# Moving the split of w_o from the scan's chunks to the w_in products, with more buffers for the chunks

## The chip, the cores and the metric

The kernel runs on one core of a Trainium2 chip. The metric is device time in microseconds (us), from the first to the last instruction of the core and what lies around it; the time before is the median of three runs.

## The reference

One decoder layer is computed for a prompt of 1024 rows and for 64 sample rows (8 sequences of 8), together T = 1088 columns. All is fp32.

```
h = rmsnorm(x) * (1 + scale) + shift                       # scale, shift, gate from silu(c) @ w_ada
[u_pool | z_pool | z_ssm | xBC | dt | g] = h @ w_in
P = (pool_mix(u_pool) * silu(z_pool)) @ w_pool_out
S = gated_rmsnorm(SSD(conv(xBC)) + D*x, z_ssm) @ w_ssm_out
x = x + gate * ((sigmoid(g_pool) * P + sigmoid(g_ssm) * S) @ w_o)
y = rmsnorm(x)
```

SSD is the scan of Mamba-2: 32 heads in 4 groups, in chunks of 128 rows, with a state that is handed from chunk to chunk. Beside y, the new pooling, convolution and scan states are written.

## The kernel before, in words

TensorE multiplies in fp32r. To keep the precision, each factor is split into a high part (a copy to fp32r by ScalarE, `act(hi, raw, AF.Copy)`) and a low part (the difference raw - hi), and each product is made of three matmuls: high by high, high by low, low by high. So each weight is split before it is used.

The stages follow each other:

- Up to about 100 us: x is normed and transposed, and the modulation is made.
- The w_in products, about 100 to 820 us. A pair of column blocks of w_in is multiplied by Strassen's scheme in seven products (`strassen`, L603 to L605). The weight blocks are split in `split`: the high part whi on ScalarE (L160), the low part wlo on GpSimd (L163), with four buffers each. Sums and differences of weights run on VectorE and GpSimd (L549), the convolution on VectorE (L1051). In the first part, the generator `splits` runs beside the products: it is stepped once a product and splits w_pool_out (8 jobs) and w_ssm_out (32 jobs, with a gain of each row put on by four ScalarE operations, L429). A job loads a 128x512 block into the tile pw (L421), makes the high half in the tile ph and stores it (L430, L431), makes the low half on GpSimd in place (L432), and stores it (L436), into tensors wp and ws in device memory. In the last part of the stage the samples' scan runs beside the products.
- The chunks, about 830 to 1110 us: 32 chunks (4 groups of 8) of the scan, between which the products with w_pool_out (`P_unit`, L1618) and w_ssm_out (`S_unit`, L1636, L1639) are woven in. The order of TensorE is written out by `in_line`; a planner orders the other engines and SyncE's queue by its own simulated times.
- The tail, from about 1110 us: the last group's products, the merge by the gates, the product with w_o (L1892 to L1894), and the last norm.

`chunk` is a generator with these steps: it loads xb (the convolved rows) and dec (the decays, L1182); makes cE and the exponentials (L1392, L1187, L1196); loads sz, transposes x and B, and makes xd (x times dt, L1412), xw and its low part xwl (the weighted x, L1415, L1419), bt and btl (B, L1406, L1420), and weighs dec and cE (L1416, L1418); then TensorE applies them (L1208, L1211) and updates the state (L1429 to L1431), and `finish` gates the result. The loop over i calls the first step three chunks ahead, the second two, the third one.

In this loop the generator `wo_splits` is stepped twice per chunk from the fourteenth chunk of the loop on, and what is left of it runs after the loop (the planner puts its instructions earlier: the first load starts at 839.9 us): 16 halves of w_o are loaded (L1668) and split (L1674, L1676), and stored to the tensors wo (L1675, L1670), from which the tail loads them. Its tile pw has two buffers, its ph one; both lie in the chunks' pools.

Tiles are named by tag, and the number of buffers of a tag is given where it is allocated. Loads are issued by SyncE (`load`), most stores by ScalarE (`store_`), each engine's queue in order: an instruction that waits holds what stands behind it. `behind` and `tc.issue_after` hold an instruction back in the planner's order until another was issued.

Of the kernel before, what the change touches and what calls it, by code (L numbers as in the profile page):

```python
# [8 lines left out]
F32 = mybir.dt.float32  # L9
F32R = mybir.dt.float32r  # L10
AF = mybir.ActivationFunctionType
ALU = mybir.AluOpType
# [8 lines left out]
P = 128  # L21
D = 1024
# [3 lines left out]
NS = 64  # L26
# [3 lines left out]
NG = 4  # L30
# [16 lines left out]
def tile_pool_ssd_step(  # L47
# [6 lines left out]
    nc = tc.nc  # L54
    uid = [0]

    def nm(s):
        uid[0] += 1
        return f"{s}_{uid[0]}"
# [325 lines left out]
    def dram(name, shape, dt=F32):  # L385
        return dr.tile(list(shape), dt, tag=name, name=name)
# [10 lines left out]
    wp_d = [dram(f"wp{m}", [P, 2, 4, P]) for m in range(8)]  # L397
    ws_d = [[dram(f"ws{g}{m}", [P, 2, 4, P]) for m in range(8)] for g in range(NG)]

    def behind(engine, n=0):  # L400

        of = (i for i in reversed(nc.cur_bb.bb.instructions) if i.engine == engine)
        for _ in range(n):
            next(of)
        return tc.issue_after(next(of))


    def splits():
        jobs = [(w_pool_out[0, :, m * P:(m + 1) * P], None, wp_d[m]) for m in range(8)]
        jobs += [(w_ssm_out[0, g * 512:(g + 1) * 512, m * P:(m + 1) * P], 24 + 4 * g, ws_d[g][m])  # L410
                 for g in range(NG) for m in range(8)]
        raws, made = {}, [0]

        def paced():

            return highs[min(made[0] + 3, len(highs) - 1)]

        def begin(n):
            raws[n] = gas[0].tile([P, 4, P], F32, tag="pw", name=nm("pw"), bufs=2)
            with tc.issue_after(paced()):  # L420
                store_(raws[n], jobs[n][0].rearrange("(k p) c -> p k c", p=P))  # L421

        def halve(n):
            raw, gain = raws[n], jobs[n][1]
            hi = gas[0].tile([P, 4, P], F32R, tag="ph", name=nm("ph"), bufs=1)
            with tc.issue_after(paced()):
                if gain is not None:
                    for k in range(4):
                        act(raw[:, k], raw[:, k], AF.Copy, scale=vT[:, gain + k:gain + k + 1])  # L429
                act(hi, raw, AF.Copy)  # L430
                store_(jobs[n][2][:, 0], hi.bitcast(F32))  # L431
            nc.gpsimd.tensor_tensor(raw.bitcast(F32R), raw, hi.bitcast(F32), ALU.subtract)  # L432

        def end(n):
            with behind(mybir.EngineType.SP):
                load(jobs[n][2][:, 1], raws.pop(n))  # L436
# [303 lines left out]
    gas = []  # L740
# [616 lines left out]
    def ckt(shape, tag, bufs=2):  # L1357
        return (cl if tag in CKL else ca if tag in ("dec", "xb", "cE") else ck).tile(list(shape), F32, tag=tag, name=nm(tag), bufs=bufs)
# [14 lines left out]
        nc.gpsimd.tensor_tensor(yl[g][:, :, o:o + S], v, yhc.bitcast(F32), ALU.subtract)  # L1373

    def sample_end(g):
        sz = ckt([P, 4, P], "sz", 3)[:, :, :NS]
        load(sz, z_d[g][:, :, SEQ:])
        v = ckt([P, 4, P], "v")[:, :, :NS]
        load(v, ys_d[g])
        finish(g, SEQ, NS, v, sz)  # L1380

    def chunk(g, c):
        o = c * P
        xb = ckt([P, 6, P], "xb", 3)
        load(xb, xbc_d[g][:, :, o:o + P])
        Bf, Cf = xb[:, 4], xb[:, 5]
        dec = ckt([P, 8, P], "dec", 3)
        decays(dec, g, c)
        yield
        if c > 0:  # L1390
# [21 lines left out]
        V.tensor_tensor(xd, pxv, dtT[:, c, heads].unsqueeze(2).to_broadcast([P, 8, 64]), ALU.mult)  # L1412
        V.tensor_tensor(pxv, pxv, wdT[:, c, heads].unsqueeze(2).to_broadcast([P, 8, 64]), ALU.mult)
        xwh, xwl = (ck.tile([P, 512], F32R, tag=t, name=nm(t), bufs=1) for t in ("xw", "xwl"))
        act(xwh, px, AF.Copy)  # L1415
        V.tensor_tensor(dec, dec, pbc[:, P:2 * P].unsqueeze(1).to_broadcast([P, 8, P]), ALU.mult)  # L1416
        if c > 0:
# [185 lines left out]
    ck = right.__enter__()  # L1603
# [54 lines left out]
                nxt += 1  # L1658
            yield from run(ws.pop(i))
    pc_ = pieces()  # L1660
    wo_d = [dram(f"wo{k}", [P, 2, D]) for k in range(8)]

    def wo_splits():
        raws = {}
        for n in range(18):
            if n < 16:
                raws[n] = ck.tile([P, 512], F32, tag="pw", name=nm("pw"), bufs=2)
                load(raws[n], w_o[0, n // 2 * P:n // 2 * P + P, n % 2 * 512:n % 2 * 512 + 512])  # L1668
            if n > 1:
                load(wo_d[(n - 2) // 2][:, 1, n % 2 * 512:n % 2 * 512 + 512], raws.pop(n - 2))  # L1670
            yield
            if n < 16:
                hi = ck.tile([P, 512], F32R, tag="ph", name=nm("ph"), bufs=1)
                act(hi, raws[n], AF.Copy)  # L1674
                store_(wo_d[n // 2][:, 0, n % 2 * 512:n % 2 * 512 + 512], hi.bitcast(F32))  # L1675
                nc.gpsimd.tensor_tensor(raws[n].bitcast(F32R), raws[n], hi.bitcast(F32), ALU.subtract)  # L1676
            yield
    wos = wo_splits()
    RATE = 2.56
    FRONT = 4  # L1680

# [11 lines left out]
        next(pc_)  # L1693
    next(seq[0])
    for i in range(len(seq)):
        if i > 12:
            next(wos, None)
        if i + 1 < len(seq):
            with behind(mybir.EngineType.DVE, 1 - i) if i < 2 else ExitStack():
                next(seq[i + 1])  # L1700
        products(i + 0.4)
        if i > 0:
            next(seq[i - 1], None)
        if i > 12:
            next(wos, None)
# [10 lines left out]
    for it in (pc_, wos):  # L1716
        for _ in it:
            pass
    in_line((mybir.EngineType.PE,))
    right.__exit__(None, None, None)  # L1720
    while right_all:
# [16 lines left out]
    for c in range(9):  # L1738
        n = min(P, T - c * P)
# [5 lines left out]
    for c in range(9):  # L1745
        n = min(P, T - c * P)
# [4 lines left out]
    wo, mh, ml = [None] * 8, [None] * 8, [None] * 8  # L1751
# [90 lines left out]
    for half in range(2):  # L1842
        c = slice(half * 512, half * 512 + 512)
# [102 lines left out]
```

## Time and profile before

| what | before |
|---|---|
| median of 3 runs | 1297.37 us (1296.57 to 1301.63) |
| span of the profiled execution | 1297.1 us |
| the profiled execution's own time around it | not given beside its span |
| TensorE busy | 1255.9 us (97%) |
| VectorE, ScalarE, GpSimd busy | 910.5, 708.8, 677.4 us |
| moved by DMA | 251.70 MB, mean 194 GB/s |

In the profile PE is TensorE, PEld its weight loads, DVE VectorE, ACT ScalarE, POOL GpSimd and SP SyncE; L12 is line 12 of the kernel, always of the kernel before in this part. A row of windows gives, for a stretch in us, its length, then the busy time of each engine with its count of instructions, the granted clock of TensorE, the share of the DMA engines and the rate in GB/s. A row of waits names who waited for whom, then the total in us, how often, and the longest. A row of a tile gives the least, the median and the greatest duration in ns, and the first and last start in us. A q behind an engine's name is its sequencer, which issues DMAs. The chain of waits lists start and duration in us.

### The profile page before, as it was taken

Reading aid. Unit: us, or ns where it says so; the run is one execution under the profiler, and the core shown is the slowest. Engines: PE = TensorE matmul, PEld = TensorE weight load, DVE = VectorE, ACT = ScalarE, POOL = GpSimd, SP = SyncE. Lnnn points to the kernel's source line nnn. Section 1 sums busy time; section 2 is a strip of 40 time slices with the busy share of each in tenths; the row PEclk is TensorE's granted clock in tenths of the full one; section 3 lists DMA queues with packets and bytes.
Section 4 is the critical chain, followed back from the end, with each engine's and each line's share of the span. In section 5 each row is a group of like instructions: output and inputs, shape, how many; then the busy total and the mean of one; then the engine's idle time right before and its main releaser. Section 6 shows DMA issues by size and latency. Waiting matters only on the chain.

```text
span 1297.1 us, 26554 instructions
## 1 busy us (share of the span) xinstructions
PE 1255.9 (97%) x9771; PEld 1173.9 (90%) x9771; DVE 910.5 (70%) x1580; ACT 708.8 (55%) x1684; POOL 677.4 (52%) x563
## 2 busy tenths in 40 slices
PE   7999999999999999999999999999998999999998
PEld 6779999989999999999889999889998999999786
DVE  4685778866979578775777665488676888576433
ACT  4665356375656564545455453687987868201111
POOL 1007668677869776664344444276776747314000
PEclk9999999999999999999999999999999999999999
DMA  9837345465455544444656555999988656575631
GB/s 326 259 107 224 119 150 173 142 202 170 146 180 197 165 155 133 161 135 129 181 158 173 152 178 164 356 355 354 338 270 262 202 168 199 172 266 159 226 106 52
DMA packets 233795, 251.70 MB, mean 194 GB/s; under 512 B 31265, under 2 KB 177905, under 8 KB 233658
## 3 DMA queue, kind: packets, MB, share of 16 engines
q1 hardware_dynamic: 161568, 171.60, 42.1%
q10 hardware_dynamic: 72098, 78.41, 17.5%
q8 instruction: 77, 1.26, 0.4%
q14 instruction: 52, 0.43, 0.1%
HBM read 167.06 MB, written 83.01 MB: 193 GB/s over the span
## 4 chain that ended last, share of the span: by engine, by line
PE 67%; issue 8%; DMA 8%; DVE 6%; POOL 5%; ACT 4%; SPq 0%; ACTq 0%; POOLq 0%; DVEq 0%
PE ps L603 6%; PE ps L604 6%; PE ps L605 6%; PE mm L603 6%; PE mm L605 6%; PE mm L604 6%; PE mm L355 3%; PE mm L356 3%; PE mm L354 3%; PE ps L1208 2%; PE ps L1892 2%; PE ps L1894 2%; PE ps L1893 2%; POOL wlo L163 2%; PE ps L1211 2%
## 5 line engine op out<-in xcount | busy, mean ns | idle before, releaser
L163 POOL TENSOR_TENSOR wlo<-rawA,whi 128x512 fp32r<-128x512 f32 x120 | 184.0, 1538 | 185.6 <-ACT whi L160 101.6
L163 POOL TENSOR_TENSOR wlo<-raw,whi 128x512 fp32r<-128x512 f32 x92 | 150.7, 1646 | 125.3 <-ACT whi L160 91.1
L354 PE MATMUL mm<-Y,whi 128*128 128x352 f32 (+1 forms) x480 | 160.1, 334 | 0.7 <-DVE G L1795 0.5
L355 PE MATMUL mm<-Y,whi 128*128 128x352 f32 (+1 forms) x480 | 157.3, 328 | 1.0 <-DVE Y L1466 1.0
L356 PE MATMUL mm<-Y,wlo 128*128 128x352 f32 (+1 forms) x480 | 156.9, 327 | 0.0
L605 PE MATMUL mm<-Y,wlo 128*128 128x272 f32 x496 | 143.6, 290 | 3.9 <-POOL wlo L163 3.1
L603 PE MATMUL ps<-Y,whi 128*128 128x272 f32 x496 | 144.5, 291 | 2.3 <-ACT o L803 1.7
L603 PE MATMUL mm<-Y,whi 128*128 128x272 f32 x496 | 146.5, 295 | 0.2
L604 PE MATMUL ps<-Y,whi 128*128 128x272 f32 x496 | 143.1, 289 | 0.0
L604 PE MATMUL mm<-Y,whi 128*128 128x272 f32 x496 | 142.9, 288 | 0.0
L605 PE MATMUL ps<-Y,wlo 128*128 128x272 f32 x496 | 142.6, 288 | 0.0
L160 ACT ACTIVATE whi<-rawA 128x512 fp32r<-128x512 f32 x125 | 78.2, 626 | 95.6 <-PE ps L604 44.9
L1051 DVE SCALAR_TENSOR_TENSOR GA<-GA,cvT,GA 128x1112 f32<-128x1112 f32 x72 | 127.1, 1769 | 0.6 <-ACT GA L1048 0.5
L160 ACT ACTIVATE whi<-raw 128x512 fp32r<-128x512 f32 x96 | 58.7, 626 | 91.4 <-DVE raw L549 41.7
L605 PEld LDWEIGHTS mm<-Y,wlo 128*128 128x128 f32 x496 | 93.4, 188 | 5.8 <-POOL wlo L163 4.2
L603 PEld LDWEIGHTS ps<-Y,whi 128*128 128x128 f32 x496 | 93.3, 188 | 4.0 <-ACT o L803 1.9
L603 PEld LDWEIGHTS mm<-Y,whi 128*128 128x128 f32 x496 | 93.3, 188 | 2.5 <-issue 0.8
L604 PEld LDWEIGHTS mm<-Y,whi 128*128 128x128 f32 x496 | 93.4, 188 | 0.7 <-issue 0.6
L604 PEld LDWEIGHTS ps<-Y,whi 128*128 128x128 f32 x496 | 93.3, 188 | 0.3 <-issue 0.2
L605 PEld LDWEIGHTS ps<-Y,wlo 128*128 128x128 f32 x496 | 93.4, 188 | 0.2 <-issue 0.2
L354 PEld LDWEIGHTS mm<-Y,whi 128*128 128x128 f32 x480 | 90.3, 188 | 3.2 <-DVE G L1795 1.4
L355 PEld LDWEIGHTS mm<-Y,whi 128*128 128x128 f32 x480 | 90.3, 188 | 3.2 <-DVE Y L1466 1.6
(452 smaller groups left out, 3851.6 us busy)
## 6 DMA issues: line engine op xcount, KB each, us to landing
rawA<-in_w_in SPq DMA_DIRECT2D x46, 512.0 KB
dec<-acs_d SPq DMA_DIRECT2D x32, 512.0 KB
xbc<-GA ACTq DMA_DIRECT2D x24, 512.0 KB
xb<-xbc SPq DMA_DIRECT2D x32, 384.0 KB
rawA<-in_w_in SPq DMA_DIRECT2D x32, 256.0 KB
pw<-in_w_ssm_out ACTq DMA_DIRECT2D x32, 256.0 KB
ws<-ph ACTq DMA_DIRECT2D x32, 256.0 KB
ws<-pw SPq DMA_DIRECT2D x32, 256.0 KB
```

Source lines behind the costliest of these rows:

```text
L160: ins = act(hi[:, :, :ncols], raw[:, :, :ncols], AF.Copy)
L163: (eng or nc.gpsimd).tensor_tensor(lo[:, :, :ncols], raw[:, :, :ncols], hi[:, :, :ncols].bitcast(F32), ALU.subtract)
L354: mm(ps[:, :n], a, rh[k][:, o:o + n], start=(k == 0), stop=False)
L355: mm(ps[:, :n], a, rl[k][:, o:o + n], start=False, stop=False)
L356: mm(ps[:, :n], b, rh[k][:, o:o + n], start=False, stop=(k == nk - 1))
L603: mm(p, hi, ah, start=(k == 0), stop=False)
L604: mm(p, hi, al, start=False, stop=False)
L605: mm(p, lo, ah, start=False, stop=(k == 3))
L1051: V.scalar_tensor_tensor(d[:, :n], rp[:, k:k + n], cvT[:, 24 * k + mc:24 * k + mc + 1], d[:, :n], ALU.mult, ALU.add)
L1208: mm(o[hh], xd[:S, 2 * q + hh, :], dec[:S, 2 * q + hh], start=True, stop=state is None)
L1211: mm(o[hh], state[:, h * 64:h * 64 + 64], cE[:, h], start=False, stop=True)
L1892: mm(ps[:, :cw], mhk, wo[k][0][:, s], start=(k == 0), stop=False)
```

## The change

The 16 halves of w_o are split by `splits`, as jobs 40 to 55 behind those of w_pool_out and w_ssm_out, beside the w_in products; `wo_splits` and its steps in the loop over chunks are taken out. The jobs are spaced 12/5 steps apart in place of 17/5, so that 56 of them end where 40 did, and the tile pw there has three buffers in place of two. In the chunks, xb, dec and sz get a fourth buffer, and xd, xw, xwl, bt and btl a second. The scratch memory that is reserved for dynamic DMAs is set to 1024 (`dynamic_dma_scratch_size`); before, it was left at its larger default.

```
     def splits():
-        jobs = [(w_pool_out[0, :, m * P:(m + 1) * P], None, wp_d[m]) for m in range(8)]
-        jobs += [(w_ssm_out[0, g * 512:(g + 1) * 512, m * P:(m + 1) * P], 24 + 4 * g, ws_d[g][m])
-                 for g in range(NG) for m in range(8)]
+        jobs = [(tiles(w_pool_out[0, :, m * P:(m + 1) * P]), None, [wp_d[m][:, j] for j in range(2)]) for m in range(8)]
+        jobs += [(tiles(w_ssm_out[0, g * 512:(g + 1) * 512, m * P:(m + 1) * P]), 24 + 4 * g,
+                  [ws_d[g][m][:, j] for j in range(2)]) for g in range(NG) for m in range(8)]
+        jobs += [(half(w_o[0, k * P:(k + 1) * P], n), None, [half(wo_d[k][:, j], n) for j in range(2)])
+                 for k in range(8) for n in range(2)]
...
-            raws[n] = gas[0].tile([P, 4, P], F32, tag="pw", name=nm("pw"), bufs=2)
+            raws[n] = gas[0].tile([P, 4, P], F32, tag="pw", name=nm("pw"), bufs=3)
...
-                at.setdefault(n * 17 // 5 + step, []).append((f, n))
+                at.setdefault(n * 12 // 5 + step, []).append((f, n))
...
     def chunk(g, c):
-        xb = ckt([P, 6, P], "xb", 3)
+        xb = ckt([P, 6, P], "xb", 4)
-        dec = ckt([P, 8, P], "dec", 3)
+        dec = ckt([P, 8, P], "dec", 4)
-        sz = ckt([P, 4, P], "sz", 3)
+        sz = ckt([P, 4, P], "sz", 4)
-        bth, btl = (ck.tile([P, P], F32R, tag=t, name=nm(t), bufs=1) for t in ("bt", "btl"))
+        bth, btl = (ck.tile([P, P], F32R, tag=t, name=nm(t), bufs=2) for t in ("bt", "btl"))
-        xd = ckt([P, 8, 64], "xd", 1)
+        xd = ckt([P, 8, 64], "xd", 2)
-        xwh, xwl = (ck.tile([P, 512], F32R, tag=t, name=nm(t), bufs=1) for t in ("xw", "xwl"))
+        xwh, xwl = (ck.tile([P, 512], F32R, tag=t, name=nm(t), bufs=2) for t in ("xw", "xwl"))
...
-    def wo_splits():
-        raws = {}
-        for n in range(18):
-            if n < 16:
-                raws[n] = ck.tile([P, 512], F32, tag="pw", name=nm("pw"), bufs=2)
-                load(raws[n], w_o[0, n // 2 * P:n // 2 * P + P, n % 2 * 512:n % 2 * 512 + 512])
-            if n > 1:
-                load(wo_d[(n - 2) // 2][:, 1, n % 2 * 512:n % 2 * 512 + 512], raws.pop(n - 2))
-            yield
-            if n < 16:
-                hi = ck.tile([P, 512], F32R, tag="ph", name=nm("ph"), bufs=1)
-                act(hi, raws[n], AF.Copy)
-                store_(wo_d[n // 2][:, 0, n % 2 * 512:n % 2 * 512 + 512], hi.bitcast(F32))
-                nc.gpsimd.tensor_tensor(raws[n].bitcast(F32R), raws[n], hi.bitcast(F32), ALU.subtract)
-            yield
...
-        if i > 12:
-            next(wos, None)
...
-    nc = _bacc.Bacc("TRN2", target_bir_lowering=False, num_devices=1)
+    nc = _bacc.Bacc("TRN2", target_bir_lowering=False, num_devices=1, dynamic_dma_scratch_size=1024)
```

`sample_end` gets the fourth sz as well. The destination of a half of w_o is the same as before, its high part by ScalarE's queue and its low part by SyncE's; its load is now issued by ScalarE.

More of the change, by code (lines that the diff above doesn't have):

```diff
@@ L398, in tile_pool_ssd_step @@
     ws_d = [[dram(f"ws{g}{m}", [P, 2, 4, P]) for m in range(8)] for g in range(NG)]
+    wo_d = [dram(f"wo{k}", [P, 2, D]) for k in range(8)]
     def behind(engine, n=0):
@@ L418, in begin @@
         def begin(n):
[L419 removed]
+            raws[n] = gas[0].tile([P, 4, P], F32, tag="pw", name=nm("pw"), bufs=3)
             with tc.issue_after(paced()):
[L421 removed]
+                store_(raws[n], jobs[n][0])
         def halve(n):
@@ L430, in halve @@
                 act(hi, raw, AF.Copy)
-                store_(jobs[n][2][:, 0], hi.bitcast(F32))
+                store_(jobs[n][2][0], hi.bitcast(F32))
             nc.gpsimd.tensor_tensor(raw.bitcast(F32R), raw, hi.bitcast(F32), ALU.subtract)
@@ L435, in end @@
             with behind(mybir.EngineType.SP):
-                load(jobs[n][2][:, 1], raws.pop(n))
+                load(jobs[n][2][1], raws.pop(n))
         at = {}
@@ L1715, in tile_pool_ssd_step @@
     next(seq[-1], None)
-    for it in (pc_, wos):
-        for _ in it:
-            pass
+    for _ in pc_:
+        pass
     in_line((mybir.EngineType.PE,))
```

10 lines of the change are left out of this document (5 added, 5 removed).

## The prediction
> **What bounds the kernel now.** I read the page first, for which engine fills the span.
>
> ```profile
> span 1297.1 us, 26554 instructions
> PE 1255.9 (97%) x9771; PEld 1173.9 (90%) x9771; DVE 910.5 (70%) x1580; ACT 708.8 (55%) x1684; POOL 677.4 (52%) x563
> ```
>
> TensorE is busy in 97% of the span. The change adds and removes no matmul, and in the built program TensorE's order is the same except for four places in the w_in products, where the two halves of one product change places. So the time can move only by TensorE's idle time: 1297.1 - 1255.9 = 41.2 us in all. Next I asked for windows over the stages that the change touches: the w_in products (100 to 560 us, with their tight stretches) and the chunks of the scan (830 to 1100 us).
>
> ```profile
> core 0: us, PE busy (x) PEld busy (x) DVE busy (x) ACT busy (x) POOL busy (x), PEclk, DMA share, GB/s
> 100.00:560.00 460.00, 453.96 (x3563) 446.10 (x3561) 347.48 (x533) 255.06 (x607) 344.16 (x219) 1.00 0.51 166
> 180.00:240.00 60.00, 59.17 (x470) 58.34 (x469) 54.14 (x74) 34.61 (x85) 50.78 (x28) 1.00 0.46 151
> 280.00:300.00 20.00, 19.66 (x155) 19.19 (x155) 14.41 (x23) 11.93 (x31) 16.63 (x11) 1.00 0.81 258
> 400.00:420.00 20.00, 20.00 (x161) 19.73 (x160) 18.43 (x25) 12.02 (x31) 18.59 (x10) 1.00 0.72 239
> 830.00:1000.00 170.00, 161.28 (x1313) 149.52 (x1312) 127.27 (x189) 139.67 (x384) 110.58 (x118) 1.00 0.97 322
> 910.00:930.00 20.00, 20.00 (x172) 18.28 (x171) 13.72 (x20) 18.72 (x53) 13.80 (x16) 1.00 1.06 382
> 1000.00:1100.00 100.00, 99.63 (x835) 92.27 (x834) 84.50 (x135) 75.13 (x206) 63.25 (x77) 1.00 0.64 189
> ```
>
> The reader is to see three things. From 830 to 1000 us TensorE idles 170.00 - 161.28 = 8.7 us; from 1000 to 1100 us, in the same loop over chunks, it idles 0.4 us. From 100 to 560 us it idles 6.0 us, with VectorE and GpSimd both near full in places (54.14 and 50.78 of 60 us). And the granted clock is 1.00 in each row, so a busier TensorE has lost no clock here.
>
> What lies between 830 and 1000 us and not behind it are the 16 halves of w_o, and the waits name them:
>
> ```profile
> PE ps L1208 <- DVE dec L1416: 3.4, 3, 1.4
> PE ps L1211 <- DVE cE L1418: 2.3, 3, 0.8
> PE ps L1429 <- DVE xwl L1419: 2.0, 1, 2.0
> PE mm L355 <- DVE Y L1466: 1.0, 1, 1.0
> ...
> L1668 SPq DMA_DIRECT2D pw<-in_w_o x16: 332/402/2769, 839.9 to 984.2; - x16
> L1674 ACT ACTIVATE ph<-pw x16: 615/624/644, 847.2 to 988.5; 128x512 fp32r<-128x512 f32 x16
> L1676 POOL TENSOR_TENSOR pw<-pw,ph x16: 1266/1292/1809, 847.9 to 989.3; 128x512 fp32r<-128x512 f32 x16
> L1670 SPq DMA_DIRECT2D wo<-pw x16: 319/354/965, 849.2 to 992.4; - x16
> ```
>
> TensorE's waits there are on VectorE, but VectorE was itself late. The chain of waits shows why in its largest case:
>
> ```profile
> 842.85 7.48 DMA xb<-xbc
> ...
> 966.53 6.14 DMA dec<-acs_d
> ...
> 974.80 0.52 ACT ph L1674
> 975.35 5.84 DMA wo<-ph
> 981.83 0.45 ACT xw L1415
> ...
> 989.83 0.69 DVE xwl L1419
> ```
>
> The tile ph has one buffer. ScalarE may not write the next half into it before the store of the last one has landed (5.84 us), and behind that instruction in ScalarE's queue stands the xw of the scan, on which VectorE's xwl and TensorE's L1429 depend. The other chains begin with a load: xb took 7.48 us, dec 6.14 us, at 322 GB/s in this stage. Traffic alone is not the cause: from 910 to 930 us the rate was 382 GB/s and TensorE idled 0.0 us. What hurts is an in-order queue that waits for a transfer.
>
> **The change part by part.**
>
> *w_o leaves the chunks.* Out of this stage go 16 ph (16 x 0.624 = 10.0 us of ScalarE), 16 differences on GpSimd (16 x 1.292 = 20.7 us), 32 DMA issues of SyncE's queue and 16 of ScalarE's, and 16 x 3 x 256 KB = 12.6 MB, which at 322 GB/s over 170 us (54.7 MB) is 23% of the traffic: about 248 GB/s stay. SyncE's loads of chunks stood behind these in its queue:
>
> ```profile
> SPq L1668 <- DMA wo<-pw: 14.0, 5, 4.6
> ...
> SPq L1670 <- POOL pw L1676: 10.1, 10, 2.4
> ...
> SPq L1182 <- PE ps L1211: 6.7, 4, 2.6
> ```
>
> 24.1 us of SyncE's waits in this stage were for w_o. The nearest row for the stage without w_o is 1000 to 1100 us: 0.37 us idle per 100, so 0.6 us in 170. Gain 8.7 - 0.6 = 8.1 us. Its ends: 2.0 us if only the one wait behind ph (L1429) goes, 8.7 us if all goes. I take 8.1, since the row compared with is the same loop. What is late next is then nothing that costs: TensorE runs at its own pace.
>
> *The further buffers.* VectorE waits for the single xd, but this is cheap:
>
> ```profile
> DVE xd L1412 <- PE ps L1208: 24.3, 14, 3.8
> ...
> DVE xd L1412 <- PE ps L1208: 10.6, 12, 1.2
> ```
>
> The first row is 860 to 1000 us, the second 1000 to 1110 us, where TensorE hardly idles in spite of twelve such waits. So I put the second xd, xw and bt at nothing beyond the 8.1 us. The fourth xb, dec and sz let SyncE issue a load one chunk earlier (the 6.7 us in which L1182 waited for L1211); the built order of SyncE puts the first chunk's loads ahead of the first wp loads. Worth 0 to 0.6 us, which is all that is left, or, if a deeper burst makes a needed weight or load late, minus one load of 7.5 us; I take 0, as the stage without w_o shows nothing to gain.
>
> *The smaller scratch.* The traffic is in these queues:
>
> ```profile
> q1 hardware_dynamic: 161568, 171.60, 42.1%
> q10 hardware_dynamic: 72098, 78.41, 17.5%
> q8 instruction: 77, 1.26, 0.4%
> q14 instruction: 52, 0.43, 0.1%
> ```
>
> The kernel's DMAs are issued by SyncE and ScalarE; no queue of GpSimd's shows. The scratch only gives room for the buffers: 0 us.
>
> *w_o enters the w_in products.* There are now 56 jobs in place of 40 over the same steps:
>
> ```profile
> L429 ACT ACTIVATE pw<-pw,vT x128: 384/387/406, 180.1 to 520.5; 128x128 f32<-128x128 f32 x128
> L430 ACT ACTIVATE ph<-pw x40: 613/624/636, 103.4 to 523.9; 128x512 fp32r<-128x512 f32 x40
> L432 POOL TENSOR_TENSOR pw<-pw,ph x40: 1272/1296/2385, 104.5 to 524.6; 128x512 fp32r<-128x512 f32 x40
> L421 ACTq DMA_DIRECT2D pw<-in_w_ssm_out x32: 386/390/668, 177.1 to 515.0; - x32
> ...
> L163 POOL TENSOR_TENSOR wlo<-rawA,whi x120: 1258/1297/2383, 99.0 to 812.2; 128x512 fp32r<-128x512 f32 x120
> ...
> PE mm L605 <- POOL wlo L163: 2.9, 5, 0.8
> ```
>
> A job came each (523.9 - 103.4)/39 = 10.8 us; 56 jobs make that 7.6 us. ScalarE gets 16 x (0.624 + 2 x 0.390) = 22.5 us more, two of its issues a job, and the scaled jobs (four L429 of 0.387 us each) come closer together. ScalarE is busy 255 of 460 us, so this hides, so long as no ph waits for its store; 7.6 us between jobs is still above the 5.84 us of the loaded stage. The DMA rate rises from 166 by 12.6 MB / 460 us = 27 to 193 GB/s: hidden. SyncE gets 16 stores more, placed behind its w_in loads.
>
> GpSimd is the one without cover. It gets 16 x 1.296 = 20.7 us, and it makes the low halves wlo of the w_in weights, for which TensorE already waited 2.9 us. The same GpSimd operation takes 1.258 us at the least and 2.383 us at the most, the long ones while VectorE works on SBUF. In the three tight stretches (100 us together) GpSimd is busy 50.78 + 16.63 + 18.59 = 86.0 us. There 100/7.6 - 100/10.8 = 3.9 more jobs come, 5.1 us at the median and 9.3 us at the longest, against 14 us idle that are not all usable. I take half of 5.1 us as reaching TensorE, 2.5 us. In the other 360 us GpSimd idles 360 - 258 = 102 us against 12.1 jobs x 1.296 = 15.7 us; four buffers of wlo cover nearly all: 0.5 us. Loss 3.0 us. Its ends: 0 if the buffers cover it, 20.7 us if each operation delays TensorE.
>
> The Trainium skill, page "SBUF — State Buffer", section "Who interferes with whom", says that GpSimd and a VectorE operation with two SBUF inputs hold one port pair in turn, the loser being blocked for the other's whole instruction. The doubling from 1.258 to 2.383 us agrees. By that rule, with a port that is already full, all 20.7 us would reach TensorE and the sum would be 1297.4 - 8.1 + 20.7 = 1310 us.
>
> **Sum.** The profiled span is 1297.1 us; the median of the runs is 1297.37, 0.3 us above, and no other time of the profiled execution is shown, so 0.3 is added. 1297.4 - 8.1 + 3.0 = 1292.3 us.
>
> **The rivals.** (a) GpSimd covers all 16 operations and the rest of the chunks' waits goes too: 1297.4 - 8.7 = 1288.7 us, and 1287.7 if the 1.0 us in which TensorE waits for the first product of the chunks' stage (L355, 820 to 830 us) goes as well. For it: 116 us of GpSimd idle in 460. Against it: the wait of 2.9 us for wlo, which shows that the order matters, not only the sum.
>
> (b) It ends slower: in the stretches where VectorE and GpSimd both are full, every further GpSimd operation delays the next wlo, and so TensorE, by its own 1.3 us. All sixteen give 1310.0 us, twelve 1304.9. It decides from the point where TensorE loses 8.1 us here, between six and seven of the sixteen operations, and is over the bound below from twelve. For it: 54.14 and 50.78 busy of 60 us. Against it: only three such stretches in the built span of 420 us, and four low halves of stock.
>
> (c) The change does not do what it says: the chunks go on waiting, since deeper loads and a new VectorE order put another wait (dec, cE) in place of those removed. Then only L1429's 2.0 us go: 1297.4 - 2.0 + 3.0 = 1298.4 us. For it: the largest row of TensorE's waits is on dec, not on ph. Against it: the same loop without w_o idles 0.4 us in 100.
>
> **How the numbers follow.** 0.5% is 6.5 us, about what a measurement of this kernel can tell from no change: under 1290.9 is faster, over 1303.9 slower. Forecast 0.50; with a loss of 0 to 6 us about the gain of 8.1 its own range is 1289.3 to 1295.3, and a third of it lies under 1290.9: 0.17 faster, 0.33 the same. (a) 0.25, faster. (b) 0.15, of which 0.14 slower and 0.01 the same. (c) 0.10, of which 0.09 the same and 0.01 slower. Together 0.42 faster, 0.43 the same, 0.15 slower. The range for 8 in 10 begins 0.8 us under (a)'s end, as the lowest run before lay 0.8 us under the median, at 1286.9, and ends at 1304.5; it leaves out most of (b).
>
> **What would show it.** Right: from 830 to 1000 us TensorE idle near 0.6 us, no wait of ScalarE for wo<-ph, no SyncE wait for w_o there; from 100 to 560 us TensorE idle near 9 us, the added part under waits for wlo. Wrong: idle over 4 us in the chunks (the step that w_o causes it), or over 14 us, or unchanged 6 us, in the w_in products (the half that I let through).

## The result, and the profile after

The changed kernel takes 1309.61 us (median of four runs, 1307.68 to 1314.52), the kernel before 1298.51 us (1296.57 to 1301.63, the first three runs and one more). The recorded ratio of the runs is 1.0103, 95% interval [1.0073, 1.0133] (the quotient of the two medians is 1.0085): slower by 1%, where 1292.3 us was forecast. The page of the changed kernel's profiled execution (1309.22 us) begins so:

```profile
span 1307.5 us, 26515 instructions
PE 1262.0 (97%) x9771; PEld 1179.4 (90%) x9771; DVE 913.1 (70%) x1580; ACT 706.6 (54%) x1684; POOL 680.3 (52%) x563
```

The span is 10.4 us longer. TensorE idles 1307.5 - 1262.0 = 45.5 us against 41.2, so 4.3 us of it is idle time; the other 6.1 us is TensorE being busy longer with the same 9771 matmuls. The windows by stage say where (the columns are those of the prediction's windows):

```profile
100.00:560.00 460.00, 449.50 (x3490) 440.19 (x3488) 345.86 (x524) 258.49 (x616) 361.69 (x219) 0.99 0.58 190
560.00:830.00 270.00, 264.57 (x2230) 246.90 (x2231) 175.22 (x398) 138.09 (x292) 124.88 (x108) 0.99 0.54 163
830.00:1000.00 170.00, 159.56 (x1279) 147.97 (x1279) 122.88 (x185) 130.63 (x360) 84.86 (x97) 0.99 0.81 265
1000.00:1100.00 100.00, 100.00 (x841) 93.59 (x841) 85.36 (x133) 74.84 (x208) 58.39 (x72) 1.00 0.62 194
```

From 100 to 560 us TensorE idles 10.5 us, before 6.0, and in that time it starts 3490 matmuls where it started 3563. From 830 to 1000 us it idles 10.4 us, before 8.7, although w_o is gone from there and the rate fell from 322 to 265 GB/s. The granted clock is 0.99 in three of the rows, where it was 1.00 before.

A cleaner measure of the two stages is the row of line L1400 (L1410 in the changed kernel), the first transposition of x in each chunk: it gives the time at which the chunks begin and the start of their last one. Before:

```profile
L1400 PE MATMUL ps<-ident,xb x128: 270/272/273, 832.8 to 1102.2; 128*128 128x128 f32 x128
```

After:

```profile
L1410 PE MATMUL ps<-ident,xb x128: 270/272/273, 843.3 to 1113.1; 128*128 128x128 f32 x128
```

The chunks begin 10.5 us later, and their stretch is 269.8 us against 269.4. So the w_in products lost the whole difference, and the chunks gained nothing where 8.1 us were expected. (The expectations below take this stretch for before and after as 269.1 and 269.5 us, by a neighbouring start.)

**In the w_in products** ScalarE's waits have changed. Before, from 100 to 560 us, these were the rows of the jobs' tiles that led:

```profile
ACT pw L429 <- DMA pw<-in_w_ssm_out: 6.9, 8, 1.9
ACT ph L430 <- DMA ws<-ph: 5.9, 3, 2.5
```

After, the same stretch and view:

```profile
ACT ph L440 <- DMA ws<-ph: 17.1, 9, 6.6
ACT pw L439 <- DMA pw<-in_w_ssm_out: 12.0, 3, 10.1
ACT ph L440 <- DMA wo<-ph: 10.6, 4, 4.0
ACT pw L439 <- DMA ws<-pw: 9.0, 2, 5.1
ACT ph L440 <- DMA pw<-in_w_o: 6.7, 2, 4.5
```

ScalarE stands 55.4 us in these five rows. The timeline of the changed kernel shows how such a wait reaches TensorE (start, duration, then in brackets the idle time just before and what ended it):

```profile
258.45 1.28 ACT L439 ACTIVATE pw<-pw,vT 128x128 f32<-128x128 f32 x4 [10.11 <-DMA pw<-in_w_ssm_out]
...
260.33 1.27 POOL L163 TENSOR_TENSOR wlo<-rawA,whi 128x512 fp32r<-128x512 f32 x1 [8.18 <-ACT whi L160]
...
264.08 0.63 ACT L440 ACTIVATE ph<-pw 128x512 fp32r<-128x512 f32 x1 [2.14 <-DMA ws<-ph]
...
265.28 0.39 PE L613 MATMUL mm<-Y,whi 128*128 128x272 f32 x1 [2.10 <-ACT whi L160]
...
266.01 2.51 POOL L163 TENSOR_TENSOR wlo<-raw,whi 128x512 fp32r<-128x512 f32 x2
...
267.33 0.59 PE L615 MATMUL mm<-Y,wlo 128*128 128x272 f32 x1 [1.54 <-POOL wlo L163]
```

ScalarE stands 10.11 us for the load of a job's pw, and again 2.14 us for the store of the single ph. Behind these in its queue is the high part whi of the w_in weights; GpSimd waits for whi (8.18 us); TensorE idles 2.10 us for whi and 1.54 us for wlo. Then comes what the prediction had not counted: after these pauses the same windows view, cut finer, shows TensorE's clock at half:

```profile
256.00:262.00 6.00, 6.00 (x40) 5.11 (x39) 4.34 (x13) 3.49 (x10) 1.27 (x1) 1.00 0.47 133
...
267.00:273.00 6.00, 5.67 (x25) 5.67 (x26) 0.00 (x0) 6.00 (x16) 5.22 (x5) 0.50 0.63 210
...
854.00:857.00 3.00, 2.61 (x9) 2.26 (x8) 2.61 (x4) 1.12 (x3) 0.00 (x0) 0.51 1.09 312
```

The records of the clock hold three such stretches ahead of the tail: 6.83 us from 266.5, 3.41 us from 676.1 and 3.41 us from 853.6. That is 13.65 us at half speed, 6.8 us lost, which accounts for the 6.1 us by which TensorE was busy longer. The kernel before had none in its profiled execution until 1293 us.

When the loss comes is told by the lag, that is, by how much later the same matmul starts than in the kernel before. By the times of the kernel before it is 2.2 us at 200 us, 6.7 us at 280 and still 6.7 us at 410, and 8.7 us at 426. In the changed kernel the first load of a half of w_o starts only at 408.7 us:

```profile
L431 ACTq DMA_DIRECT2D pw<-in_w_o x16: 339/340/616, 408.7 to 524.7; - x16
```

So most of the loss came while the first forty jobs ran, closer together than before, ahead of w_o's own.

**In the chunks** TensorE's waits have other names, and two of them are larger than any before (830 to 1000 us):

```profile
PE ps L1218 <- DVE dec L1426: 4.1, 2, 3.9
PE ps L1412 <- DVE xwl L1429: 2.7, 1, 2.7
PE ps L1221 <- DVE hst L1448: 1.4, 2, 0.8
```

The first is the 3.9 us ahead of 852.8 us. The timeline shows that VectorE had stood for a load of the products with w_pool_out, and that the scan's xd was queued behind it:

```profile
832.03 0.53 SPq L1395 DMA_DIRECT2D xb<-xbc  x1
...
841.56 0.42 SPq L1625 DMA_DIRECT2D R<-gp  x1
...
845.83 0.56 DVE L1628 TENSOR_TENSOR R<-mm,R 128x384 f32<-128x384 f32 x1 [3.88 <-DMA R<-gp]
...
849.32 0.68 DVE L1422 TENSOR_TENSOR xd<-ps,dtT 128x512 f32<-128x512 f32 x1
...
851.48 1.22 DVE L1426 TENSOR_TENSOR dec<-dec,ps 128x1024 f32<-128x1024 f32 x1 [0.77 <-ACT bt L1416]
```

With the fourth buffers SyncE issues the third chunk's xb (832.03) and dec ahead of this R (841.56). The run xb_dec_sz_3 below shows the other order.

### The profile page after: what moved, and what is told of

Its sections match the earlier page's. It is cut to its first block, busy times and chain, and to the rows that moved or that the text cites. A ratio compares the mean times of both kernels' runs of the same rounds, so it can differ in the third digit from the quotient of the medians.

```text
span 1307.5 us, 26515 instructions
## 1 busy us (share of the span) xinstructions
PE 1262.0 (97%) x9771; PEld 1179.4 (90%) x9771; DVE 913.1 (70%) x1580; ACT 706.6 (54%) x1684; POOL 680.3 (52%) x563
## 4 chain that ended last, share of the span: by engine, by line
PE 51%; DMA 5%; DVE 4%; ACT 3%; issue 3%; POOL 2%; ACTq 0%; SPq 0%; DVEq 0%; POOLq 0%
PE mm L354 4%; PE mm L356 4%; PE mm L355 4%; PE ps L613 4%; PE ps L614 3%; PE ps L615 3%; PE mm L613 3%; PE mm L614 3%; PE mm L615 3%; PE ps L1879 2%; PE ps L1881 2%; PE ps L1880 2%; PE ps L1218 2%; PE ps L1221 1%; PE ps L1299 1%
## 5 line engine op out<-in xcount | busy, mean ns | idle before, releaser
L163 POOL TENSOR_TENSOR wlo<-rawA,whi 128x512 fp32r<-128x512 f32 x120 | 180.6, 1509 | 181.0 <-ACT whi L160 103.4
L163 POOL TENSOR_TENSOR wlo<-raw,whi 128x512 fp32r<-128x512 f32 x92 | 153.8, 1680 | 105.4 <-ACT whi L160 99.5
L442 POOL TENSOR_TENSOR pw<-pw,ph 128x512 fp32r<-128x512 f32 x56 | 93.8, 1674 | 29.4 <-ACT ph L440 24.8
L613 PEld LDWEIGHTS mm<-Y,whi 128*128 128x128 f32 x496 | 93.7, 189 | 5.6 <-ACT whi L160 4.0
L1206 ACT ACTIVATE dec<-dec,acT 128x128 f32<-128x128 f32 (+1 forms) x288 | 86.8, 386 | 17.5 <-POOL dec L1197 14.1
L614 PEld LDWEIGHTS mm<-Y,whi 128*128 128x128 f32 x496 | 93.8, 189 | 0.7 <-issue 0.6
```

The source lines that it names most:

```text
L163: (eng or nc.gpsimd).tensor_tensor(lo[:, :, :ncols], raw[:, :, :ncols], hi[:, :, :ncols].bitcast(F32), ALU.subtract)
L613: mm(p, hi, ah, start=(k == 0), stop=False)
L614: mm(p, hi, al, start=False, stop=False)
L1206: act(dec[:, h], dec[:, h], AF.Exp, bias=acT[:S, c, 8 * g + h:8 * g + h + 1], scale=-1.0)
```

## The experiments

Each ratio is to the runs of the kernel before on the same chip. "Begin" is the start of the chunks less 832.8 us, "stretch" the time from there to the start of the last one (269.4 us before); both are from one profiled execution each, from the row of L1400 or its counterpart.

| kernel | us, median | ratio, 95% interval | begin, us | stretch, us |
|---|---|---|---|---|
| changed | 1309.61 | 1.0103 [1.0073, 1.0133] | +10.5 | 269.8 |
| ph2 | 1307.65 | 1.0068 [1.0044, 1.0091] | +8.6 | 271.2 |
| short_pool | 1311.54 | 1.0093 [1.0057, 1.0129] | +9.2 | 268.7 |
| bufs_only | 1307.84 | 1.0062 [1.0042, 1.0082] | +0.8 | 277.5 |
| move_only | 1306.31 | 1.0064 [1.0040, 1.0089] | +12.7 | 269.5 |
| pace_only | 1324.21 | 1.0183 [1.0158, 1.0208] | +15.8 | 280.2 |
| xb_dec_sz_3 | 1304.30 | 1.0036 [1.0013, 1.0059] | +13.6 | 260.7 |
| beside_samples | 1326.73 | 1.0206 [1.0180, 1.0232] | +30.4 | 264.3 |
| beside_samples_bufs | 1332.28 | 1.0238 [1.0211, 1.0264] | +30.4 | 271.2 |
| scratch_only | 1309.26 | 1.0079 [1.0054, 1.0105] | -0.1 | 276.9 |
| deep_jobs | 1287.85 | 0.9917 [0.9886, 0.9947] | -3.5 | 261.5 |
| deep_jobs_xb4 | 1298.19 | 0.9998 [0.9979, 1.0016] | -2.2 | 268.9 |
| deep_move | 1293.20 | 0.9971 [0.9951, 0.9991] | -3.8 | 266.1 |

**short_pool**, the changed kernel with GpSimd's share of the sixteen jobs cut to 1/128 of the elements (the rest of the low halves of w_o is left out):

```
-            nc.gpsimd.tensor_tensor(raw.bitcast(F32R), raw, hi.bitcast(F32), ALU.subtract)
+            s = slice(0, 4 if n < 40 else 1)
+            c = slice(0, P if n < 40 else 4)
+            nc.gpsimd.tensor_tensor(raw[:, s, c].bitcast(F32R), raw[:, s, c], hi[:, s, c].bitcast(F32), ALU.subtract)
```

> The changed kernel in which the GpSimd differences of the 16 jobs of w_o are made on 1/128 of each tile only (the low half of w_o stays mostly unsplit), so that GpSimd gains 16 operations of some 0.1 us in place of 1.3 to 2.4. Theory P: TensorE's loss in the w_in products goes back to that of before, idle 6 to 7 us from 100 to 560 us, time 1300 to 1303 us. Theory Q: ScalarE's waits stay, idle 9 us or more there, 1306 to 1311 us.

Its window shows GpSimd relieved and TensorE not:

```profile
100.00:560.00 460.00, 449.53 (x3492) 440.06 (x3490) 338.85 (x524) 258.42 (x616) 340.20 (x219) 0.99 0.58 190
```

GpSimd is busy 340.20 us in place of 361.69, TensorE idles 10.5 us as in the changed kernel, and the chunks begin 9.2 us late against 10.5. GpSimd's work on the sixteen halves isn't what costs. The run doesn't reach the prediction's 2.5 us in the tight stretches, though: these end at 420 us, and up to there the jobs are nearly all those of w_pool_out and w_ssm_out, which keep their whole GpSimd work here. For these, deep_jobs below gives the answer. By short_pool the rule that the prediction quoted from the Trainium skill (page "SBUF — State Buffer", section "Who interferes with whom") does not decide here: its time of 1310 us came out, but not by its mechanism.

**ph2**, the changed kernel with a second ph:

```
-            hi = gas[0].tile([P, 4, P], F32R, tag="ph", name=nm("ph"), bufs=1)
+            hi = gas[0].tile([P, 4, P], F32R, tag="ph", name=nm("ph"), bufs=2)
```

> The changed kernel with a second buffer for ph in the w_in products, nothing else. Theory Q (queue): TensorE lost its 8.7 us by 560 us because ScalarE, which issues in order, stood waiting for the store of the last ph (31 us of waits in 100 to 560 us against 9 before), so whi and then wlo came late. Then ScalarE's waits for a store of ph fall under 10 us, TensorE idles 6 to 8 us from 100 to 560 us in place of 10.5, the clock keeps 1.0 there, and the time is 1301 to 1305 us. Theory P (port): the 16 further differences on GpSimd are what delays wlo. Then nothing changes: 1307 to 1311 us, TensorE idle 9 us or more.

The waits for ph's stores went, and at 280 us the lag was 1.3 us, not 6.7 us as in the changed kernel. But the loads of pw stayed late, the jobs that had been held back came in a heap, and one new stall took most of it back. ScalarE's and then GpSimd's work ahead of it in the timeline:

```profile
390.39 1.27 ACT L439 ACTIVATE pw<-pw,vT 128x128 f32<-128x128 f32 x4
...
394.37 4.06 POOL L442 TENSOR_TENSOR pw<-pw,ph 128x512 fp32r<-128x512 f32 x2
398.38 3.59 POOL L163 TENSOR_TENSOR wlo<-raw,whi 128x512 fp32r<-128x512 f32 x2
```

GpSimd did two jobs' differences in 4.06 us ahead of the wlo that TensorE needed; TensorE idled 2.98 us, the clock fell to half for 6.83 us, and the lag was 7.0 us at 426. By the figures named beforehand this run came out as the port theory had it: 1307.65 us, and TensorE idle 9.3 us from 100 to 560 us. The waits went as the queue theory had it, but not the time, so one more buffer was not enough to tell the queue from the work.

**pace_only**, the kernel before with closer jobs and the small scratch (w_o stays in the chunks):

```
-                at.setdefault(n * 17 // 5 + step, []).append((f, n))
+                at.setdefault(n * 12 // 5 + step, []).append((f, n))
```

> The kernel before with one edit in the planner of the first splits: the 40 jobs of w_p and w_ssm come at 12/5 steps apart in place of 17/5 (a job each 7.6 us and not each 10.8), and the small scratch. No half of w_o is moved, the tiles pw 2 and ph 1 stay, the chunks stay. Theory Q (closeness): the single ph is written again before its store has landed, so ScalarE's queue stands for stores and loads, late high and low halves of the w_in weights make TensorE idle, and the clock falls after the idle; then TensorE is 3 to 9 us behind the kernel before by 440 us and the time is 1301 to 1307 us, ScalarE waits over 12 us for ws<-ph. Theory N (number): it is the sixteen further jobs that cost, closeness alone does not; then the lag at 440 us is under 2 us and the time is 1297 to 1301.

Forty jobs, none added, and the lag was 16.3 us at 426 and the time 1324.21 us, both more than the upper end expected. The small scratch does not explain it: with it alone (scratch_only) the kernel is 2.0 us ahead at 426. So the closeness, with two pw and one ph, is enough for the loss, without any further job. ScalarE's largest wait from 100 to 560 us:

```profile
ACT pw L429 <- DMA pw<-in_w_ssm_out: 37.7, 19, 5.8
```

With two pw a load can be issued only when the job before the last has been stored, and it is issued by ScalarE's own queue; ScalarE then waits for it. The chunks lost 10.8 us as well, of which scratch_only has 7.5 below.

**move_only** and **bufs_only** split the change: the first is the changed kernel with the chunks' buffers as before, the second the kernel before with the small scratch and the further buffers except those of bt and btl.

```
move_only, against the changed kernel; so too sz, xb, xwl, bt, btl:
-        dec = ckt([P, 8, P], "dec", 4)
+        dec = ckt([P, 8, P], "dec", 3)
-        xd = ckt([P, 8, 64], "xd", 2)
+        xd = ckt([P, 8, 64], "xd", 1)
bufs_only, against the kernel before: the same lines the other way round, but not bt, btl
```

> The changed kernel with the chunks' buffers as before: only w_o is moved. The loss in the w_in products is the same as in the changed kernel (8 to 9 us by 560 us) by both theories. Theory O: without the further buffers the chunks take 261 to 263 us from the first to the last transposes in place of 269.5, and the time is 1300 to 1304 us. Theory N: the two stalls have another cause, the chunks keep 268 to 270 us, and the time is 1307 to 1311 us.

> The kernel before with the smaller scratch and the further buffers of xb, dec, sz, xd, xw and xwl (not bt and btl, for which there is no room), w_o split in the chunks as before. Theory N (the buffers change nothing): 1296 to 1300 us, the chunks' waits for w_o's store stay. Rival O (the order that the planner makes with more buffers puts VectorE's xd and the loads late and brings the stalls of 3.9 and 2.7 us seen after the change): 1302 to 1307 us, with TensorE's wait for dec or xwl at the start of the chunks.

move_only shows the loss in the w_in products whole (12.7 us, of which 1.0 was there at 100 us) and no gain in the chunks (269.5 us). bufs_only shows none in the w_in products, and 8.1 us lost in the chunks, with stalls of 4.67 and 3.21 us on dec (L1416). At this point I took this for the further buffers' doing.

**scratch_only**, the kernel before with the smaller scratch and nothing else, showed that this reading was wrong:

```
-    nc = _bacc.Bacc("TRN2", target_bir_lowering=False, num_devices=1)
+    nc = _bacc.Bacc("TRN2", target_bir_lowering=False, num_devices=1, dynamic_dma_scratch_size=1024)
```

> The kernel before with the small scratch alone; every run so far had it. Its built order is the same on TensorE, but the planner puts the first loads and splits of w_o, and VectorE's and ScalarE's instructions in the chunks, at other places, since the freed memory takes the chunks' tiles earlier. Theory S (the scratch is free, as the prediction had it): 1297 to 1300 us, the chunks' stretch 268 to 270 us. Theory O (the new order by itself costs): stalls on dec L1416 as in the runs with the old place of w_o and the small scratch (further buffers only, closeness only), the chunks' stretch 275 to 281 us and the whole 1303 to 1309; then the run with the further buffers alone showed the scratch's cost, not that of the buffers.

The scratch alone costs 0.8%, and the row of the chunks shows 7.5 us of it:

```profile
L1400 PE MATMUL ps<-ident,xb x128: 270/272/273, 832.7 to 1109.6; 128*128 128x128 f32 x128
```

TensorE's instructions are in the same order, but those of the other engines are not. The memory that comes free lets the planner begin w_o's splits earlier: the first load of w_o starts at 810.24 us, before at 839.93. The timeline of ScalarE and SyncE in scratch_only shows what this pushes back:

```profile
810.24 0.70 SPq L1668 DMA_DIRECT2D pw<-in_w_o  x1
...
822.02 0.47 SPq L1182 DMA_DIRECT2D dec<-acs_d  x1
...
824.86 0.61 ACT L1674 ACTIVATE ph<-pw 128x512 fp32r<-128x512 f32 x1
...
838.64 2.13 ACT L1196 ACTIVATE dec<-dec,acT 128x128 f32<-128x128 f32 x7
...
841.04 1.22 DVE L1416 TENSOR_TENSOR dec<-dec,ps 128x1024 f32<-128x1024 f32 x1 [6.29 <-ACT bt L1406]
```

The second chunk's dec is loaded at 822.02 us (before 818.10), its exponentials (L1196) run at 838.64 (before 832.90), and TensorE idles 4.07 us at 838.2 and 5.38 us at 860.1 for dec. So w_o's first load is 29.7 us earlier and stands among the scan's first loads, and the loop over chunks costs more with nothing in it changed but the order. That w_o's instructions, among all those that moved, are what makes dec late is read from this timeline; it was not tried by itself. bufs_only's 277.5 us are thus those of the scratch; its buffers added nothing to 276.9.

**beside_samples** and **beside_samples_bufs** put the sixteen jobs beside the samples' scan, with the first forty 17/5 steps apart and w_o's in tiles pwo and pho of their own; the second has a second xd, xw, xwl and bt:

```
+    post = splits(40, 56, 140, pa, ("pwo", "pho"))
...
+        next(post, None)
```

> The sixteen halves of w_o are split neither beside the w_in products nor in the chunks, but between them, beside the samples' scan (from its step 140 on, 17/5 steps apart, in tiles of their own); the first 40 jobs stand 17/5 apart as in the kernel before, the chunks' buffers are those before, small scratch. If the place in the w_in products is what cost 8.7 to 10.5 us: the lag at 560 us is under 1.5 us. If w_o was what held the chunks up (the prediction's step of 8.1 us), the chunks' stretch takes 261 to 264 us in place of 269.1 and the whole 1290 to 1294 us. If the chunks go on waiting by their own order, as in the run with w_o moved and the old buffers, the stretch takes 268 to 270 us and the whole 1297 to 1301.

> As the run with w_o beside the samples' scan, with a second xd, xw, xwl and bt; xb, dec and sz stay at 3. Theory L: the second buffers cost nothing and the time is within 2 us of that run. Theory V: VectorE's new order brings a stall of over 2 us into the chunks, and the time is 3 to 9 us above that run.

The first answer is as expected: with the old pace the lag is 0.1 us at 523 us, and the stretch of the chunks is 5.1 us shorter. The time is not: 1290 to 1294 us were expected, and the samples' scan pays 30 us, in eleven pauses of 1.3 to 2.9 us for whi, wlo and the scan's own steps, and eight stretches of 3.41 us at half clock among them. The second kernel went against the expectation that second buffers cost nothing: the stretch is 6.9 us longer, with pauses of 3.39 and 2.59 us for btl. What puts btl late in that order was not followed further.

**xb_dec_sz_3**, the changed kernel with three xb, dec and sz:

```
-        dec = ckt([P, 8, P], "dec", 4)
+        dec = ckt([P, 8, P], "dec", 3)
```

> The changed kernel with xb, dec and sz back at 3 buffers; xd, xw, xwl and bt keep the second one, w_o stays beside the w_in products. Theory L (loads' order): the fourth buffers let SyncE put chunk loads ahead of the wp and gp loads, and this made the stall of 3.9 us at 848 us; without them the chunks' stretch takes 264 to 266 us in place of 269.5, and the whole 1304 to 1306 us. Theory V (VectorE's order): the stalls come from VectorE's in-order queue however the loads are ordered, since the second xd and xw reorder it; then the stretch stays at 268 to 271 us, the stall at about 848 us may move but one of over 2 us stays, and the time is 1307 to 1311.

```profile
L1410 PE MATMUL ps<-ident,xb x128: 270/272/273, 846.4 to 1107.1; 128*128 128x128 f32 x128
```

The stretch falls to 260.7 us, 8.7 us less than before: here is a gain of the size that was forecast. The time is at the lower end of the range expected and not below it, since in the profiled execution 13.6 us were lost by the time the chunks began. SyncE's queue and VectorE's first xd in this run:

```profile
842.84 0.32 SPq L1625 DMA_DIRECT2D R<-gp  x1
...
847.09 0.68 DVE L1422 TENSOR_TENSOR xd<-ps,dtT 128x512 f32<-128x512 f32 x1
...
850.45 0.52 SPq L1395 DMA_DIRECT2D xb<-xbc  x1
```

The third chunk's xb now comes behind this R, and VectorE waits for no load of R. In VectorE's queue this xd stands behind one step of R's sum (L1628) that follows the load and not behind three, so VectorE's order moved with that of the loads, and the two are not told apart.

**deep_jobs**, that kernel with six pw and four ph for the jobs:

```
-            raws[n] = gas[0].tile([P, 4, P], F32, tag="pw", name=nm("pw"), bufs=3)
+            raws[n] = gas[0].tile([P, 4, P], F32, tag="pw", name=nm("pw"), bufs=6)
...
-            hi = gas[0].tile([P, 4, P], F32R, tag="ph", name=nm("ph"), bufs=1)
+            hi = gas[0].tile([P, 4, P], F32R, tag="ph", name=nm("ph"), bufs=4)
```

> The changed kernel with xb, dec and sz at 3, and in the w_in products six tiles pw and four ph for the 56 jobs in place of three and one, so that no job waits for a store of the job before. Theory Q (ScalarE's queue stands for the jobs' stores and loads, and the w_in weights behind it come late): ScalarE's waits for ws<-ph, wo<-ph and ws<-pw from 100 to 560 us go from some 45 us to under 5, the lag against the kernel before at 560 us falls from 8.8 to under 3 us, the chunks keep their gain of 8 us, and the time is 1290 to 1297 us. Theory W (the work itself: ScalarE's and GpSimd's further 22 and 21 us are too much between the tight products): the waits go but the lag at 560 us stays at 6 to 10 us and the time at 1301 to 1306.

1287.85 us: 0.8% faster than the kernel before, ratio 0.9917 [0.9886, 0.9947], and the fastest of all. Its page and windows:

```profile
span 1285.5 us, 26527 instructions
PE 1256.4 (98%) x9771; PEld 1175.8 (91%) x9771; DVE 918.7 (71%) x1580; ACT 708.0 (55%) x1684; POOL 691.0 (54%) x563
```

```profile
100.00:560.00 460.00, 456.77 (x3586) 449.07 (x3585) 358.39 (x538) 262.30 (x624) 379.15 (x236) 1.00 0.60 194
...
830.00:1000.00 170.00, 168.24 (x1397) 156.37 (x1398) 133.02 (x203) 135.05 (x377) 94.69 (x107) 1.00 0.79 252
```

The same 56 jobs at the same pace, GpSimd busier than ever (379.15 of 460 us), and TensorE idles 3.2 us from 100 to 560 us where the changed kernel idled 10.5. No wait of ScalarE on a DMA for ph or pw is left in that stretch. What ScalarE does there is told by its groups (count, then busy time and mean ns, then the idle time ahead of them):

```profile
L439 ACT ACTIVATE pw<-pw,vT 128x128 f32<-128x128 f32 x128 | 41.6, 388 | 0.9 <-issue 0.9
...
L440 ACT ACTIVATE ph<-pw 128x512 fp32r<-128x512 f32 x56 | 34.7, 620 | 0.3
```

All 56 ph with 0.3 us of idle time ahead of them: the work was never too much, only the waits in front of it. The time is below the 1290 to 1297 us expected. This kernel and xb_dec_sz_3 differ in the counts of pw and ph alone, though the planner's order can move with them. In the chunks TensorE's row has the gain as well:

```profile
L1410 PE MATMUL ps<-ident,xb x128: 270/272/273, 829.3 to 1090.8; 128*128 128x128 f32 x128
```

**deep_jobs_xb4**, the same with four xb, dec and sz:

```
-        dec = ckt([P, 8, P], "dec", 3)
+        dec = ckt([P, 8, P], "dec", 4)
```

> As deep_jobs, with xb, dec and sz at 4 as in the changed kernel: the fourth buffers seen a second time. Theory L (they make SyncE's order bad): the chunks' stretch is 6 to 10 us longer than in deep_jobs, with a stall of over 2.5 us on dec near 845 us, and the time 5 to 10 us above that of deep_jobs. If the difference between the changed kernel and the one with 3 was an accident of the order, the two are within 3 us.

10.3 us slower than deep_jobs, of which the stretch has 7.4 us, and the stall is there at 836.1 us:

```profile
PE ps L1218 <- DVE dec L1426: 4.6, 2, 4.5
```

So the stall of the changed kernel at 848 us goes with the fourth buffers, in both pairs of kernels that differ in nothing else.

**deep_move**, deep_jobs with single xd, xw, xwl, bt and btl:

```
-        xd = ckt([P, 8, 64], "xd", 2)
+        xd = ckt([P, 8, 64], "xd", 1)
```

> As deep_jobs (w_o beside the w_in products, six tiles pw and four ph, small scratch, xb, dec and sz at 3), but with the chunks' xd, xw, xwl, bt and btl single as in the kernel before: the second buffers taken away alone. Theory B (the second buffers are what lets the chunks gain once w_o is gone): the chunks' stretch takes 267 to 270 us as in the run with w_o moved and the old buffers, and the time is 1294 to 1299. Theory R (w_o's going is enough, and the half clock for 7.7 us in that earlier run was an accident): the stretch takes 260 to 264 us and the time is 1286 to 1291. In both, the lag at 560 us stays under 1 us.

By the medians, on another chip, 5.4 us slower than deep_jobs, between the two theories: the stretch is 266.1 us. Of 7.9 us that deep_jobs gains there, w_o's going alone brings 3.3 and the second buffers, in this order, the other 4.6; 1.7 of these 4.6 us are a stretch of 3.41 us at half clock, at 853.3, behind a pause of 1.75 us for dec.

## Why the prediction was wrong, step by step

- **What bounds the kernel** held: only TensorE's pauses moved the time. But "the time can move only by TensorE's idle time" left out the clock. Some pauses are followed by half clock, and this was 6.1 of the 10.4 us.
- **w_o leaves the chunks, 8.1 us**: in the changed kernel the stretch gained nothing (269.8 us against 269.4). The size came out in xb_dec_sz_3 (8.7) and deep_jobs (7.9), where TensorE idles 1.9 and 1.8 us from 830 to 1000 us (0.6 forecast), but not by the step as stated: without the second xd, xw and bt, which were put at nothing, w_o's going brought -0.1, 3.3 and 5.1 us (move_only, deep_move, beside_samples). With them a third kernel lost 1.8 us (beside_samples_bufs). That the sum's term is near 8 us in two kernels is therefore partly luck.
- **The further buffers, 0**: this step failed. The fourth xb, dec and sz cost 7.4 us (deep_jobs_xb4) to 9.1 us (changed against xb_dec_sz_3) of the stretch, and so ate the gain. The prediction had named the way ("a deeper burst makes a needed weight or load late") with a price of 7.5 us, and took 0 since the stage without w_o showed nothing to gain. That argues against a gain, and says nothing about a loss. Rival (c), that the chunks go on waiting in a new order, is what happened there.
- **The smaller scratch, 0**: failed as an argument. The queues carried nothing of GpSimd's, true, but the memory set free changed the order of all engines but TensorE: by itself it costs 0.8%. In the changed kernel w_o no longer stands in the chunks, so that form of the loss is not in its sum; deep_jobs has the same scratch and gains. No run has the changed kernel with the larger scratch.
- **w_o enters the w_in products, ScalarE's 22.5 us hidden "so long as no ph waits for its store"**: the step that failed most, 8.7 us of lag at 523 us and 10.5 at the chunks' begin, where 0 was put. The condition was right and was judged by means: 7.6 us between jobs against a store of 5.84 us. The jobs' instructions wait in ScalarE's queue behind each other and their own loads, so they come unevenly, and the waits grew from 5.9 us to 17.1 for ws<-ph alone. The load of pw was left out of the step altogether, and so was that the closer spacing strikes the first forty jobs, by which 6.7 us were lost at 280 us, long ahead of any half of w_o.
- **GpSimd, 3.0 us**: short_pool excludes the sixteen differences as the cost; for the closer jobs ahead of them it is deep_jobs, with 379 us of GpSimd's work in 460 and TensorE idle 3.2 us there. The true price is too small to see. Rival (b) gave 1310.0 us, which is nearly the time, for a reason that these two runs exclude: that was luck.
- **What would show it**: the chunks' idle time over 4 us (it was 10.4) was named as wrong for "the step that w_o causes it". The runs say otherwise: the fourth buffers brought a new stall. From 100 to 560 us TensorE idled 10.5 us, near the 9 forecast, but not as forecast: the rise under waits for wlo is 1.8 us (4.7 against 2.9) and under whi 2.4 (2.8 against 0.4), and the half clock is not in idle time at all. As a sign that near 9 would be right, it misled.
- **The chances**: of the range 1289.3 to 1295.3 the part under 1290.9 is 1.6 of 6.0 us, 27% and not a third.

With w_in's cost at 0 and the chunks at 7.9 us, the sum's own form gives 1297.4 - 7.9 = 1289.5 us; deep_jobs measured 1287.85, with its chunks beginning 3.5 us earlier, for which the sum has no term.

Open remain: why the second buffers cost 6.9 us of the stretch in beside_samples_bufs and bring 4.6 in deep_jobs, which of xb, dec and sz makes the order worse, and why w_o's going alone is worth -0.1 us in one kernel and 5.1 in another; none of these was tried apart.

## What to carry to other kernels

When work is moved beside a tight stage, count its buffers ahead of its busy time: the engine that runs it in order stands for each load and store of a tile that comes round too early, and the moved jobs need as many buffers as jobs fit into one trip of load, work and store. A change of buffers or of free memory is a change of order wherever a planner places the instructions; price it by the built order, each load that moves ahead of another, and never at nothing because no engine needs it. And where a part of a change brings its gain and the whole does not, take the parts apart before giving up: the counts of two sets of buffers (pw and ph up, xb, dec and sz down) were all that stood between 1309.61 and 1287.85 us.

## What the runs showed of the hardware

TensorE's clock fell to half after short pauses: for 3.41 us at 624.0 after a pause of 1.53 us (xb_dec_sz_3), for 3.41 us at 926.7 after one of 1.62 us (move_only), for 6.83 us at 266.5 after a pause of 2.10 us and in the next one of 1.54 us (changed). The length of the pause does not decide it: the kernel before paused 2.40 us at 663.9 and 2.05 us at 981.1 with no loss, and the same pause near 660 us was followed by half clock in deep_jobs and not in deep_move. All these stretches last 3.41 or 6.83 us, so one costs 1.7 or 3.4 us beside the pause itself.

What decides it in these traces is where the pause falls. In each execution all changes of the clock lie whole multiples of 3.413 us apart (in the changed kernel full clock lasts 402.77 us, 118 times that, and 174.08 us, 51 times). Cut along this grid, the fourteen profiled executions have 37 pieces at full clock up to 1130 us in which TensorE idles over 1.9 us, and half clock follows all 37; of 35 pieces with 1.5 to 1.9 us it follows 13, and of the others, over 4400 with less, none. In deep_jobs the 1.98 us from 659.8 lie in one piece; in deep_move the 2.39 us from 660.8 are parted by an edge at 662.1, and so are the 2.40 us of the kernel before, at 665.3 (counted back from its one change, at 1293.4). In the tail, between 1130 and 1170 us, the clock also fell four times with no pause on record ahead of it. So the same kernel can lose or keep some us by the place of its pauses on this grid, and a difference of 1.7 or 3.4 us between two single executions above can be no more than that.

The Trainium skill, page "TensorE: Matmul & The Clock Gate", Part 1, has a free-running window of 3413 ns, which agrees with the lengths and the grid, and half rate after at least one idle window of about 3.4 us, which these runs do not bear out: a window of which about half was idle was enough.
